# Where the pre-added weight blocks of a seven-product SwiGLU pair are made: accumulating DMA or VectorE

## The chip, the cores and the metric

One core of one Trainium2 chip runs the whole program. The metric is device time in microseconds. TensorE (PE) multiplies, VectorE (DVE) and ScalarE (ACT) do elementwise work, GpSimd (POOL) also issues the accumulating DMAs, and SyncE (SP) issues the plain ones.

## The reference

Two layers on x of 512 tokens by 1024 channels, each followed by a SwiGLU feed-forward network. The change lies in the latter alone:

```python
def swiglu_layer(x, norm_g, w_gate_up, w_down):
    h = rmsnorm(x, norm_g)
    g, u = jnp.split(h @ w_gate_up, 2, axis=-1)
    return x + (jax.nn.silu(g) * u) @ w_down
```

The hidden width is 2816, which is 22 blocks of 128 columns. A block m of gate columns with the same block of up columns is called a pair here.

## The kernel before

Activations lie with channels on partitions and the 512 tokens in the free dimension. Every product is made in three matmuls: a weight is split into a rounded high part (`whi`, a cast on ACT, L93) and a remainder (`wlo`, a subtraction on VectorE, L94), and so is the activation.

In each of the two feed-forward networks pairs 0 to 4 are multiplied plainly. Pairs 5 to 21 go through `seven`: gate and up weights of a pair are seen as a 2x2 block matrix (two halves of the 1024 input channels by gate and up), the tokens as two halves, and the 2x2 product is made with seven block products instead of eight, each 4 channel blocks by 3 matmuls of 256 columns, so 84 matmuls a pair. The blocks that are needed on the weight side are, with g and u the gate and up weights and 1 and 2 their halves along the channels:

- a1: g whole, as it comes (tile `raw`);
- s13: two sums side by side, u1 + u2 and u1 + g1;
- s24: (u1 + u2) + g1, and that + g2, made by two adds on VectorE (L143, L144; called add 2 and add 3 below) out of the first half of s13 and `raw`;
- a22: u2.

Each of the four is then split into high and low parts. `emit` asks for the pieces one pair ahead: the call of `seven` for pair m makes those of pair m+1. The 17 pairs are worked in three runs, 5 to 7, 8 to 14 and 15 to 21, and after each run comes the down projection of the hidden blocks made so far (8 output blocks of 512-column matmuls). The two longer runs of both networks are called stages A (pairs 8 to 14, first network), B (15 to 21), C and D (the same of the second network).

The wide buffers are few: four weight tiles named `raw` are shared by a pair's transfers and by the down projection's weights, five high/low pairs hold split weights. So a transfer waits until the buffer that it takes has been read to the end by the pair before the last. All waiting is on queues that work in order: SP issues the plain transfers in the order of the program, POOL the accumulating ones, and VectorE and ACT also take one instruction after another, so that one which waits holds up all behind it. That order is set by the framework's scheduler when the program is built.

In `seven` VectorE also takes products out of PSUM: u2 = r2 + s (L792) has to be read before the third group of products adds to the same bank, and likewise u3 (L799), then the outputs `tg` (L807), `tu` (L812, L813). PE takes the groups of a pair in the order a1, then the rest of the pair before (s24), s24, the rest of the pair before (a22), s13, s13, a1; a group of 12 matmuls each.

In a profile row the tile that holds s13 is named `raw` before the change, since it comes out of the same ring, and a22 is shown as `a`.

Of the kernel before, what the change touches and what calls it, by code (L numbers as in the profile page):

```python
# [10 lines left out]
F32 = mybir.dt.float32  # L11
# [3 lines left out]
ALU = mybir.AluOpType  # L15
AX = mybir.AxisListType

P = 128
# [7 lines left out]
KF = FF // P  # L26
# [3 lines left out]
NSTD = 5  # L30
# [31 lines left out]
def trunk(ctx: ExitStack, tc: tile.TileContext, a):  # L62
    nc = tc.nc
    mm = nc.tensor.matmul
    V, S, G = nc.vector, nc.scalar, nc.gpsimd
# [18 lines left out]
    WMAX = D  # L84
# [7 lines left out]
    def split(src, hi, lo, eng=V):  # L92
        S.copy(hi, src)  # L93
        eng.tensor_tensor(out=lo, in0=src, in1=hi.bitcast(F32), op=ALU.subtract)  # L94
# [4 lines left out]
    lent = {"stage": None, "pool": None, "raw": 0, "split": 0}  # L99

    def ring(what, stage):

        own, more = (NRAW, 1) if what == "raw" else (NSPL, 2)
        names = (("raw", F32),) if what == "raw" else (("whi", F32R), ("wlo", F32R))
        pool, bufs = wp, own
        if stage is not None and stage == lent["stage"]:
            lent[what] += 1
            if lent[what] % (own + more) >= own:
                pool, bufs = lent["pool"], more
        return [pool.tile([P, WMAX], dt, tag=n, bufs=bufs, name=n) for n, dt in names]  # L110

    parts = {}

    def emit(j):
        src, n, kind, stage = specs[j]
        HW = WMAX // 2
        if kind == "plain":
            raw, = ring("raw", stage)
            hi, lo = ring("split", stage)
            step = n if j else n // 4  # L120
            for c in range(0, n, step):
                nc.sync.dma_start(out=raw[:, c:c + step], in_=src[:, c:c + step])
                split(raw[:, c:c + step], hi[:, c:c + step], lo[:, c:c + step], G if src.tensor.name in on_pool else V)
        elif kind == "a1":

            g, u = src
            fp = lent["pool"]
            raw, = ring("raw", stage)
            s13, = ring("raw", stage)
            a22 = fp.tile([P, HW], F32, tag="a22", name="a22", bufs=2)  # L130
            for z in range(2):
                nc.sync.dma_start(out=s13[:, z * HW:(z + 1) * HW], in_=u[:, :HW])
            nc.sync.dma_start(out=raw, in_=g)
            nc.sync.dma_start(out=a22, in_=u[:, HW:])
            nc.gpsimd.dma_start(out=s13[:, :HW], in_=u[:, HW:], accum_op=ALU.add)  # L135
            nc.gpsimd.dma_start(out=s13[:, HW:], in_=g[:, :HW], accum_op=ALU.add)
            parts.update(raw=raw, s13=s13, a22=a22)
            hi, lo = ring("split", stage)
            split(raw, hi, lo)
        elif kind == "s24":  # L140
            raw, s13 = parts["raw"], parts["s13"]
            t = lent["pool"].tile([P, WMAX], F32, tag="s24", name="s24", bufs=1)
            V.tensor_tensor(out=t[:, :HW], in0=s13[:, :HW], in1=raw[:, :HW], op=ALU.add)  # L143
            V.tensor_tensor(out=t[:, HW:], in0=t[:, :HW], in1=raw[:, HW:], op=ALU.add)  # L144
            hi, lo = ring("split", stage)
            split(t, hi, lo)
        elif kind == "s13":
            hi, lo = ring("split", stage)
            split(parts["s13"], hi, lo)
        else:  # L150
            hi, lo = (lent["pool"].tile([P, HW], F32R, tag=f"a22{z}", name=f"a22{z}", bufs=1) for z in "hl")
            split(parts["a22"], hi, lo)
        w_of[j] = (hi, lo)

    def weight(i):
        while emitted[0] < len(specs) and emitted[0] <= i + (AHEAD if specs[emitted[0]][2] == "plain" else 4):
            emitted[0] += 1
            emit(emitted[0] - 1)
        return w_of.pop(i, None)
# [69 lines left out]
    def slot(i, dtype):  # L229
        return [xp.tile([P, T], dtype, tag=f"x{z}{i}", name=f"x{z}{i}") for z in "hl"]  # L230
# [79 lines left out]
    with ExitStack() as rctx:  # L310
# [63 lines left out]
        for c in range(NT):  # L374
# [33 lines left out]
            out=adt.rearrange("p (c h) -> p c h", c=NT),  # L408
            in0=dt.rearrange("p (c h) -> p c h", c=NT),
            scalar=-1.0,  # L410
            in1=ea.rearrange("p (o h) -> p o h", o=1).to_broadcast([P, NT, H]),
# [24 lines left out]
        for g in range(2):  # L436
# [7 lines left out]
            for c in range(NT):  # L444
                s = slice(c * P, (c + 1) * P)
# [3 lines left out]
                out=t.rearrange("p (c l) -> p c l", c=NT), in0=ps.rearrange("p (c l) -> p c l", c=NT),  # L449
                in1=tri.rearrange("p (o l) -> p o l", o=1).to_broadcast([P, NT, P]), op=ALU.mult,  # L450
# [245 lines left out]
        op = rctx.enter_context(tc.tile_pool(name="op", bufs=1))  # L696
# [9 lines left out]

    HOMES = [("F", i) for i in range(5)] + [("S", i) for i in (8, 9, 10, 11, 4, 5, 6, 7)] + [("F", i) for i in range(5)] + [("S", i) for i in (8, 9, 10, 11)]

# [4 lines left out]
    def ffn(norm, idx, after):  # L717
        l, gu, dn = idx
        HT = T // 2
        with ExitStack() as fctx:  # L720
            fp = fctx.enter_context(tc.tile_pool(name="fp", bufs=1))
# [47 lines left out]
            def finish(m, tu):  # L769
                z, i = HOMES[m]  # L770
                hi, lo = slot(i, F32R) if z == "S" else [fp.tile([P, T], F32R, tag=f"a{y}{i}", name=f"a{y}") for y in "hl"]
                split(tu, hi, lo)
                act[m] = (hi, lo)

            def small(tag):
                return fp.tile([P, HT], F32, tag=tag, name=tag, bufs=2)

            def seven(m, last):

# [2 lines left out]
                r1, r2 = (pa.tile([P, T], F32, tag="pa", name="ps_r")[:, :HT] for _ in range(2))  # L782
                r3 = pm.tile([P, T], F32, tag="pm", name="ps_r3")[:, :HT]
                s, u2, u3, m5 = small("s"), small("u2"), small("u3"), small("m5")
                a1 = weight(gu[m]["a1"])
                product(r1, a1, 0, "B11", True)
# [379 lines left out]
```

## Time and profile before

| | |
|---|---|
| median of 3 runs | 1334.52 us (1334.01 to 1335.09) |
| the profiled execution | 1333.48 us, of which the span 1331.6 us |
| PE busy | 1296.0 us, 97% of the span |
| VectorE busy | 928.1 us, 70% |
| ACT busy | 645.6 us, 48% |
| POOL busy | 180.0 us, 14% |
| granted TensorE clock, mean | 0.996 |
| accumulating DMAs issued by POOL | 68 of 256 KB, median 5.5 us to landing |
| plain DMAs of gate and up weights issued by SP | 54 of 512 KB at 3.6 us, 68 of 256 KB at 3.4 us, 34 of 256 KB at 3.9 us |

The span runs from the first to the last instruction. A share of busy time is a mean over stages with different limits, and idle time on an engine costs nothing unless another waits for it in the end. In the windows below the first row is the first run of pairs, and stages A to D follow; (x) is a count of instructions. A row's duration includes pipelining: matmuls start before the one ahead has ended, so the distance between starts tells the pace.

### The profile page before, as it was taken

Reading aid. Unit: us, or ns where it says so; the run is one execution under the profiler, and the core shown is the slowest. Engines: PE = TensorE matmul, PEld = TensorE weight load, DVE = VectorE, ACT = ScalarE, POOL = GpSimd, SP = SyncE. Lnnn points to the kernel's source line nnn. Section 1 sums busy time; section 2 is a strip of 40 time slices with the busy share of each in tenths; the row PEclk is TensorE's granted clock in tenths of the full one; section 3 lists DMA queues with packets and bytes.
Section 4 is the critical chain, followed back from the end, with each engine's and each line's share of the span. In section 5 each row is a group of like instructions: output and inputs, shape, how many; then the busy total and the mean of one; then the engine's idle time right before and its main releaser. Section 6 shows DMA issues by size and latency. Waiting matters only on the chain.

```text
span 1331.6 us, 18948 instructions
## 1 busy us (share of the span) xinstructions
PE 1296.0 (97%) x7346; PEld 1113.9 (84%) x7346; DVE 928.1 (70%) x1550; ACT 645.6 (48%) x1012; POOL 180.0 (14%) x178
## 2 busy tenths in 40 slices
PE   7999989999999999999999999999999999999998
PEld 6877767788889889889888877877878989889997
DVE  6886789975688558747764666777789746765772
ACT  6743858443455325424443467546654514433540
POOL 0000000000010111011104453354201011111100
PEclk9999989999999999999999999999999999999999
DMA  7323322532454646564632321221245554565541
GB/s 242 112 80 94 96 74 70 163 111 91 143 131 109 173 109 164 162 143 111 158 96 80 95 79 33 64 79 49 66 132 120 158 127 127 144 162 131 148 128 56
DMA packets 58154, 153.46 MB, mean 115 GB/s; under 512 B 6464, under 2 KB 7232, under 8 KB 57936
## 3 DMA queue, kind: packets, MB, share of 16 engines
q1 hardware_dynamic: 48272, 134.43, 32.7%
q0 software_dynamic: 9792, 17.83, 8.6%
q8 instruction: 57, 0.93, 0.3%
q14 instruction: 33, 0.27, 0.1%
HBM read 150.10 MB, written 2.13 MB: 114 GB/s over the span
## 4 chain that ended last, share of the span: by engine, by line
PE 81%; DVE 8%; ACT 4%; DMA 4%; issue 2%; SPq 0%; POOL 0%; DVEq 0%; ACTq 0%; POOLq 0%
PE ps_pr L163 15%; PE ps_pr L164 15%; PE ps_pr L165 15%; PE ps_r L765 6%; PE ps_r L767 6%; PE ps_r L766 6%; DMA raw<-in_w_gu 4%; PE ps_qkv L905 3%; PE ps_qkv L906 3%; PE ps_qkv L907 3%; DVE wlo L94 3%; PE ps_pT L1017 1%; ACT s L996 1%; PE ps_s L988 1%; PE ps_o L1025 1%
## 5 line engine op out<-in xcount | busy, mean ns | idle before, releaser
L93 ACT CAST whi<-raw 128x1024 fp32r<-128x1024 f32 (+2 forms) x223 | 227.4, 1022 | 327.1 <-PE ps_pr L165 208.8
L163 PE MATMUL ps_pr<-xh,wlo 128*128 128x512 f32 x704 | 279.7, 397 | 13.0 <-DVE wlo L94 12.3
L164 PE MATMUL ps_pr<-xl,whi 128*128 128x512 f32 x704 | 277.7, 394 | 0.6 <-DVE xl L245 0.6
L165 PE MATMUL ps_pr<-xh,whi 128*128 128x512 f32 x704 | 276.6, 393 | 0.0
L94 DVE TENSOR_TENSOR wlo<-raw,whi 128x1024 fp32r<-128x1024 f32 (+2 forms) x191 | 224.4, 1181 | 42.1 <-ACT whi L93 41.2
L163 PEld LDWEIGHTS ps_pr<-xh,wlo 128*128 128x128 f32 x704 | 133.5, 190 | 42.4 <-DVE wlo L94 13.1
L164 PEld LDWEIGHTS ps_pr<-xl,whi 128*128 128x128 f32 x704 | 133.4, 189 | 29.7 <-DVE xl L245 1.8
L165 PEld LDWEIGHTS ps_pr<-xh,whi 128*128 128x128 f32 x704 | 133.3, 189 | 28.6 <-issue 0.6
L840 DVE TENSOR_TENSOR x<-ps_pr,x 128x512 f32<-128x512 f32 x48 | 33.2, 691 | 96.8 <-PE ps_pr L165 96.6
L94 POOL TENSOR_TENSOR wlo<-raw,whi 128x1024 fp32r<-128x1024 f32 x32 | 78.0, 2438 | 167.1 <-ACT whi L93 167.1
L135 POOL DMA_DIRECT2D raw<-in_w_gu x34 | 30.4, 893 | 482.8 <-DMA raw<-in_w_gu 191.8
L765 PE MATMUL ps_r<-xh,wlo 128*128 128x256 f32 x272 | 77.1, 283 | 0.0
L767 PE MATMUL ps_r<-xh,whi 128*128 128x256 f32 x272 | 77.0, 283 | 0.0
L766 PE MATMUL ps_r<-xl,whi 128*128 128x256 f32 x272 | 77.0, 283 | 0.0
L907 PE MATMUL ps_qkv<-whi,xh 128*128 128x512 f32 x192 | 75.5, 393 | 0.0
L905 PE MATMUL ps_qkv<-whi,xl 128*128 128x512 f32 x192 | 75.4, 392 | 0.0
L906 PE MATMUL ps_qkv<-wlo,xh 128*128 128x512 f32 x192 | 75.3, 392 | 0.0
L93 ACT CAST whi<-s 128x1024 fp32r<-128x1024 f32 x34 | 35.8, 1052 | 71.2 <-PE ps_pr L165 37.4
L143 DVE TENSOR_TENSOR s<-raw 128x512 f32<-128x512 f32 x34 | 23.5, 691 | 56.3 <-DMA raw<-in_w_gu 54.5
L163 PE MATMUL ps_pr<-ah,wlo 128*128 128x512 f32 x160 | 62.3, 389 | 0.0
L164 PE MATMUL ps_pr<-al,whi 128*128 128x512 f32 x160 | 62.3, 389 | 0.0
L165 PE MATMUL ps_pr<-ah,whi 128*128 128x512 f32 x160 | 62.2, 389 | 0.0
(372 smaller groups left out, 3074.7 us busy)
## 6 DMA issues: line engine op xcount, KB each, us to landing
raw<-in_w_gu SPq DMA_DIRECT2D x54, 512.0 KB, 3.6
raw<-in_w_in SPq DMA_DIRECT2D x35, 512.0 KB, 3.6
raw<-in_w_gu SPq DMA_DIRECT2D x68, 256.0 KB, 3.4
raw<-in_w_gu POOLq DMA_DIRECT2D x68, 256.0 KB, 5.5
raw<-in_w_dn SPq DMA_DIRECT2D x32, 448.0 KB, 3.9
raw<-in_w_qkv SPq DMA_DIRECT2D x24, 512.0 KB, 3.5
a<-in_w_gu SPq DMA_DIRECT2D x34, 256.0 KB, 3.9
raw<-in_w_out SPq DMA_DIRECT2D x16, 512.0 KB, 3.6
```

The costliest lines, as they stand in the source:

```text
L93: S.copy(hi, src)
L94: eng.tensor_tensor(out=lo, in0=src, in1=hi.bitcast(F32), op=ALU.subtract)
L163: mm(ps, lhsT=wl[ws], rhs=xh[xs], start=start, stop=False)
L164: mm(ps, lhsT=wh[ws], rhs=xl[xs], start=False, stop=False)
L165: mm(ps, lhsT=wh[ws], rhs=xh[xs], start=False, stop=stop)
L765: mm(ps, lhsT=wl[:, c:c + P], rhs=fh, start=first and k == 0, stop=False, skip_group_check=not first)
L766: mm(ps, lhsT=wh[:, c:c + P], rhs=fl, start=False, stop=False, skip_group_check=not first)
L767: mm(ps, lhsT=wh[:, c:c + P], rhs=fh, start=False, stop=k == 3, skip_group_check=not first)
L840: V.tensor_tensor(out=x[m], in0=ps, in1=x[m], op=ALU.add)
L905: mm(pss[t], lhsT=xl[:, ts_], rhs=wh[:, cols], start=(k == 0), stop=False)
L906: mm(pss[t], lhsT=xh[:, ts_], rhs=wl[:, cols], start=False, stop=False)
L907: mm(pss[t], lhsT=xh[:, ts_], rhs=wh[:, cols], start=False, stop=(k == KD - 1))
```

## The change

The sum u1 + u2 is made on VectorE out of a plain transfer of the whole u tile (`up`, from the same ring as `raw`); the accumulating DMA is left for u1 + g1 alone. The s13 tile has two buffers of its own. The add on VectorE is called add 1. u2 has no buffer of its own any more: a22 is the second half of `up`, which is therefore held until a22 has been split. To make room, a pair of hidden blocks fewer is kept in that pool (`HOMES` tells in which buffer a hidden block lies) and three small tiles have one buffer instead of two.

```diff
         elif kind == "a1":
 
             g, u = src
-            fp = lent["pool"]
             raw, = ring("raw", stage)
-            s13, = ring("raw", stage)
-            a22 = fp.tile([P, HW], F32, tag="a22", name="a22", bufs=2)
-            for z in range(2):
-                nc.sync.dma_start(out=s13[:, z * HW:(z + 1) * HW], in_=u[:, :HW])
+            up, = ring("raw", stage)
+            s13 = lent["pool"].tile([P, WMAX], F32, tag="s13", name="s13", bufs=2)
+            nc.sync.dma_start(out=s13[:, HW:], in_=u[:, :HW])
             nc.sync.dma_start(out=raw, in_=g)
-            nc.sync.dma_start(out=a22, in_=u[:, HW:])
-            nc.gpsimd.dma_start(out=s13[:, :HW], in_=u[:, HW:], accum_op=ALU.add)
+            nc.sync.dma_start(out=up, in_=u)
             nc.gpsimd.dma_start(out=s13[:, HW:], in_=g[:, :HW], accum_op=ALU.add)
-            parts.update(raw=raw, s13=s13, a22=a22)
+            a22 = up[:, HW:]
+            parts.update(raw=raw, s13=s13, a21=up[:, :HW], a22=a22)
             hi, lo = ring("split", stage)
             split(raw, hi, lo)
         elif kind == "s24":
             raw, s13 = parts["raw"], parts["s13"]
+            V.tensor_tensor(out=s13[:, :HW], in0=parts["a21"], in1=parts["a22"], op=ALU.add)
             t = lent["pool"].tile([P, WMAX], F32, tag="s24", name="s24", bufs=1)
...
-    HOMES = [("F", i) for i in range(5)] + [("S", i) for i in (8, 9, 10, 11, 4, 5, 6, 7)] + [("F", i) for i in range(5)] + [("S", i) for i in (8, 9, 10, 11)]
+    NF = NSTD - 1
+    HOMES = [("F", i) for i in range(NF)] + [("S", i) for i in (8, 9, 10, 11, 4, 5, 6, 7)] + [("F", i) for i in range(3)]
+    HOMES += [("S", i) for i in (8, 9, 10, 11)] + [("F", i) for i in range(NF)]
+    assert len(HOMES) >= KF
...
             def small(tag):
-                return fp.tile([P, HT], F32, tag=tag, name=tag, bufs=2)
+                return fp.tile([P, HT], F32, tag=tag, name=tag, bufs=2 if tag == "s" else 1)
```

The scheduler puts the instructions in another order. The first place is SP's queue in stage A, where it issues for pairs 12 to 14. Before, L133 is a gate tile (raw_4619 and raw_4754 are those of pairs 13 and 14), L132 the two halves of s13 (raw_4485, raw_4620 and raw_4755: pairs 12, 13 and 14), L134 a22:

```order
L134 DMA a22_4351<-in_w_gu 128x512
L132 DMA raw_4485<-in_w_gu 128x512 x2
L132 DMA raw_4620<-in_w_gu 128x512 x2
L134 DMA a22_4486<-in_w_gu 128x512
L133 DMA raw_4754<-in_w_gu 128x1024
L133 DMA raw_4619<-in_w_gu 128x1024
L134 DMA a22_4621<-in_w_gu 128x512
L132 DMA raw_4755<-in_w_gu 128x512 x2
```

In the same place of the changed program L131 is a gate tile (raw_4611 and raw_4745 for pairs 13 and 14), L132 the whole up tile (raw_4344, raw_4478, raw_4612 and raw_4746: pairs 11 to 14), and L130 the u1 half that the accumulating DMA then adds to:

```order
L131 DMA raw_4477<-in_w_gu 128x1024
L132 DMA raw_4344<-in_w_gu 128x1024
L130 DMA s13_4479<-in_w_gu 128x512
L132 DMA raw_4478<-in_w_gu 128x1024
L131 DMA raw_4611<-in_w_gu 128x1024
L130 DMA s13_4613<-in_w_gu 128x512
L131 DMA raw_4745<-in_w_gu 128x1024
L132 DMA raw_4612<-in_w_gu 128x1024
L130 DMA s13_4747<-in_w_gu 128x512
L132 DMA raw_4746<-in_w_gu 128x1024
```

A pair's three plain transfers take the place of four, and the whole up tile of a pair is issued before or after its neighbour's gate tile, as its buffer comes free.

The second place is VectorE's queue at the end of the same stage, where the last pair's s24 is made (add 2 and add 3 of pair 14 are L143 and L144) beside the split of pair 13's s13 (wlo_4698):

```order
L143 TENSOR_TENSOR s24_4794<-raw_4755,raw_4754 128x512
L94 TENSOR_TENSOR xl6_4694<-tu_4476,xh6_4693 128x512
L799 TENSOR_TENSOR u3_4617<-ps_r_4613,s_4615 128x256
L144 TENSOR_TENSOR s24_4794<-s24_4794,raw_4754 128x512
L800 TENSOR_TENSOR tu_4611<-m5_4618,u3_4617 128x256
L94 TENSOR_TENSOR wlo_4798<-s24_4794,whi_4797 128x1024
L94 TENSOR_TENSOR wlo_4698<-raw_4620,whi_4697 128x1024
L807 TENSOR_TENSOR tg_4610<-ps_r3_4614,u2_4616 128x256
L94 TENSOR_TENSOR wlo_4764<-raw_4754,whi_4763 128x1024
```

After the change add 1 of pair 14 is L140, add 2 and add 3 are L142 and L143, and wlo_4689 is the split of pair 13's s13:

```order
L94 TENSOR_TENSOR a22l_4586<-raw_4478,a22h_4585 128x512
L814 TENSOR_TENSOR tu_4469<-ps_r_4471,s_4473 128x256
L815 SCALAR_TENSOR_TENSOR tu_4469<-tu_4469,tg_4468 128x512
L140 TENSOR_TENSOR s13_4747<-raw_4746 128x512
L801 TENSOR_TENSOR u3_4609<-ps_r_4605,s_4607 128x256
L94 TENSOR_TENSOR xl7_4685<-tu_4469,xh7_4684 128x512
L802 TENSOR_TENSOR tu_4603<-m5_4610,u3_4609 128x256
L142 TENSOR_TENSOR s24_4784<-s13_4747,raw_4745 128x512
L143 TENSOR_TENSOR s24_4784<-s24_4784,raw_4745 128x512
L94 TENSOR_TENSOR wlo_4689<-s13_4613,whi_4688 128x1024
L94 TENSOR_TENSOR wlo_4788<-s24_4784,whi_4787 128x1024
L809 TENSOR_TENSOR tg_4602<-ps_r3_4606,u2_4608 128x256
```

The add that waits for a transfer is now add 1, it stands further ahead of the splits, and pair 13's s13 is split ahead of pair 14's s24 instead of behind it.

## Rows read from the trace of the kernel before

**Rows 1.** The page, busy time of TensorE over the whole span
```profile
PE 1296.0 (97%) x7346; PEld 1113.9 (84%) x7346; DVE 928.1 (70%) x1550; ACT 645.6 (48%) x1012; POOL 180.0 (14%) x178
```

**Rows 2.** Windows (start:end, length, busy PE, PEld, DVE, ACT, POOL, clock, DMA, GB/s)
```profile
413.20:443.43 30.23, 30.23 (x253) 30.23 (x252) 23.53 (x34) 17.00 (x26) 0.00 (x0) 1.00 0.43 126
486.98:560.20 73.22, 71.05 (x589) 70.64 (x588) 55.10 (x85) 37.94 (x61) 7.04 (x8) 1.00 0.58 150
598.31:673.69 75.38, 72.27 (x589) 70.97 (x588) 54.87 (x85) 37.49 (x61) 7.07 (x8) 1.00 0.51 131
1101.41:1177.27 75.86, 72.96 (x590) 72.14 (x589) 55.08 (x85) 37.40 (x61) 7.07 (x8) 0.98 0.54 137
1215.37:1289.69 74.32, 71.82 (x589) 70.80 (x588) 55.02 (x85) 38.02 (x61) 7.06 (x8) 1.00 0.58 144
```

**Rows 3.** Timeline of TensorE: first matmul of a run, first one after it
```profile
413.20 0.28 PE L765 MATMUL ps_r<-b110h,wlo 128*128 128x256 f32 x1
...
443.43 0.40 PE L163 MATMUL ps_pr<-ah,wlo 128*128 128x512 f32 x1
```

**Rows 4.** Timeline, stage A: pair 14's pieces, until TensorE goes on
```profile
527.04 2.35 DVE L94 TENSOR_TENSOR wlo<-raw,whi 128x1024 fp32r<-128x1024 f32 x2
...
528.28 0.80 SPq L132 DMA_DIRECT2D raw<-in_w_gu  x2
...
531.53 0.89 POOL L135 DMA_DIRECT2D raw<-in_w_gu  x1 [16.34 <-DVE tu L812]
...
536.64 0.69 DVE L143 TENSOR_TENSOR s<-raw 128x512 f32<-128x512 f32 x1 [3.72 <-DMA raw<-in_w_gu]
537.25 0.68 DVE L94 TENSOR_TENSOR xl<-tu,xh 128x512 fp32r<-128x512 f32 x1
...
538.98 1.05 ACT L93 CAST whi<-s 128x1024 fp32r<-128x1024 f32 x1 [5.73 <-PE ps_r L767]
539.93 1.04 ACT L93 CAST whi<-raw 128x1024 fp32r<-128x1024 f32 x1
...
541.20 1.22 DVE L94 TENSOR_TENSOR wlo<-raw,whi 128x1024 fp32r<-128x1024 f32 x1
542.33 0.42 DVE L807 TENSOR_TENSOR tg<-ps_r,u 128x256 f32<-128x256 f32 x1
542.47 0.39 PE L765 MATMUL ps_r<-t00h,wlo 128*128 128x256 f32 x1 [2.06 <-DVE wlo L94]
542.67 1.21 DVE L94 TENSOR_TENSOR wlo<-raw,whi 128x1024 fp32r<-128x1024 f32 x1
```

**Rows 5.** What VectorE waited for in stages A, B, C, D
```profile
DVE s L143 <- DMA raw<-in_w_gu: 8.5, 4, 3.7
DVE wlo L94 <- ACT whi L93: 4.1, 8, 0.9
...
DVE s L143 <- DMA raw<-in_w_gu: 12.7, 4, 5.4
...
DVE s L143 <- DMA raw<-in_w_gu: 10.9, 4, 4.5
...
DVE s L143 <- DMA raw<-in_w_gu: 10.7, 4, 4.8
```

**Rows 6.** Window in stage C in which the granted clock was lower
```profile
1149.50:1152.90 3.40, 3.40 (x17) 3.19 (x16) 2.05 (x5) 0.89 (x2) 0.00 (x0) 0.50 0.77 243
```

**Rows 7.** The line of the 512 KB gate transfers, and that of add 2
```profile
DMA to landing us min/median/max: 3.4/3.9/6.6
...
L143 DVE TENSOR_TENSOR s<-raw x34: 680/692/694, 398.1 to 1267.1; 128x512 f32<-128x512 f32 x34
```

**Rows 8.** Timeline of VectorE ahead of the first run of pairs
```profile
391.64 0.69 DVE L830 TENSOR_TENSOR tu<-ps_pr,nrb 128x512 f32<-128x512 f32 x1 [0.59 <-PE ps_pr L165]
...
413.40 0.69 DVE L830 TENSOR_TENSOR tu<-ps_pr,nrb 128x512 f32<-128x512 f32 x1 [0.91 <-PE ps_pr L165]
...
416.54 0.41 DVE L792 TENSOR_TENSOR u<-ps_r,s 128x256 f32<-128x256 f32 x1
```

## The prediction

> **What bounds the kernel now.** I read the page's busy times first. TensorE is busy for 1296.0 us of 1331.6, so some 35 us are open at most by that line [rows 1]. Next I looked for the stages in which it loses them, with the starts of its matmuls. The first run of three pairs goes from 413.20 to 443.43 without a gap: 30.23 us for 3 x 84 = 252 matmuls, 0.120 us each, 10.08 us a pair [rows 2, 3]. Seven pairs at that pace are 70.54 us. The four stages of seven pairs take 73.22, 75.38, 75.86 and 74.32 us [rows 2]: 2.68 + 4.84 + 5.32 + 3.78 = 16.6 us too much. That is all that a change of how the weight blocks are made can give back here.
>
> What the stages wait for I read from stage A's timeline [rows 4]. A split of s13 frees its buffer (VectorE's two subtractions from 527.04), SP issues the two u1 halves of pair 14 at 528.28, POOL the first accumulate at 531.53, once they have landed, and add 2 of pair 14 can start at 536.64: 8.4 us from SP's issue, behind an idle VectorE. Behind add 2 stands add 3, then ACT's cast of s24 at 538.98, and only behind that, in ACT's order, the cast of pair 13's s13 at 539.93, its subtraction at 541.20, and TensorE at 542.47 after 2.06 us of idleness. VectorE's waits for transfers at add 2 are 8.5, 12.7, 10.9 and 10.7 us in the stages, 42.8 us in 16 waits, 2.7 us each [rows 5]. In stage C such a wait also brings a stretch of 3.4 us at a granted clock of 0.50 (1.2 GHz instead of 2.4) [rows 6], half of which is lost; it is part of the 16.6 us.
>
> **The change part by part.** *The accumulate ahead of s24 goes.* s24 then needs only plain transfers. The accumulate that is left feeds the second half of s13, and that is split about two pairs after its buffer came free, 20 us, against the 8.4 us that both transfers took above: nothing is late there. I cost it at nothing; without that cover it would be the stall of rows 4 again.
>
> *What is late next* is `up`. By the changed program's waits it takes the buffer that one of three VectorE instructions frees (split of a22, split of a1, or add 3, of an earlier pair), is issued by SP at once unless another transfer ahead of it in the queue waits, and lands, if it behaves like the gate tile of the same size, 3.9 us later [rows 7]. VectorE meanwhile works on what its order puts between. At the pace of the rows, 0.60 us for a 512-column instruction (536.64 to 537.25), 1.13 for a split of 1024, 0.34 for 256 columns (541.20, 542.33, 542.67) [rows 4], that is, for pairs 11 to 14 in A and C and 18 to 21 in B and D, five times 3.1 us, three times 1.3, twice 2.4, twice 3.4, twice 4.6, once 2.2 and once 3.0. So add 1 waits five times 0.8, three times 2.6, twice 1.5, twice 0.5, twice not at all, once 1.7, once 0.9: 18.4 us in place of 42.8. Queued behind a waiting add 1 are u3, the outputs' split, add 2 and add 3, and the split of s13 or a1; the first that TensorE needs is s13's subtraction, 5.8 us into its pair, and u2, 7.2 us into it.
>
> What these waits cost TensorE is not in the trace, so from both sides. Nothing, if they end inside VectorE's slack: I put stage A's instructions of the changed order one behind another with these durations, and each split and u2 came before TensorE's need, the nearest by 0.4 us (u2 of pair 13). At the most, in proportion as before: 16.6 / 42.8 = 0.39 us of TensorE time for one of VectorE's waiting, 0.39 x 18.4 = 7.1 us. I take the middle, 3.6 us, since the transfers won't all land in 3.9.
>
> *34 more adds.* Each is an add like L143, 0.69 us [rows 7]. In the stages VectorE is busy for (55.10 + 54.87 + 55.08 + 55.02) / 28 = 7.86 us a pair [rows 2]; with the add 8.55 of 10.08. Its waits for ACT's casts, at the most-loaded kind of stage 4.1 us or 0.6 a pair [rows 5], leave about 0.9 us. So the adds lie beside TensorE's work, and cost nothing as long as add 1 waits for no more than that on average. Ahead of the first run of each network VectorE is nearly full: add 1 of three pairs and an a22 split that moves ahead are 4 x 0.6 = 2.4 us, against idle pieces of 0.59 and 0.91 [rows 8], so up to 0.9 us late at u2 of pair 5. That u2 starts at 416.54 and TensorE needs it by 417.5 (a run's first pair has nothing of a pair before it between its groups, so the group that needs u2 read begins after three groups of 12 matmuls: 413.20 + 3 x 1.44), done at 416.95 [rows 8]. Between 0 and 0.9 us I take 0.2, near to nothing, twice: 0.4 us.
>
> *The rest* costs nothing: u2, u3 and m5 with one buffer are read by VectorE half a pair before they are written again; the hidden blocks' new homes were all read by an earlier down projection; SP issues one transfer less per pair and POOL one of two.
>
> The sum, against the profiled execution's 1333.48 us: - 16.6 + 3.6 + 0.4 = - 12.6, so 1320.9. The median of the runs is 1.04 us above that execution: 1322 us.
>
> The Trainium skill ("Perfetto Trace Analysis", section "Identifying the Most-Contended Engine") holds that matmul occupancy is a poor measure of how much TensorE has left, because pipelined instructions look smaller in a trace. By occupancy the four stages hold 2.17 + 3.11 + 2.90 + 2.50 = 10.7 us of idleness, by the pace of starts 16.6 us [rows 2]; by the first the sum would be 1328, by the second it is 1322. The trace agrees with the rule in that a slow matmul counts as busy: the 3.4 us at half clock are wholly busy [rows 6].
>
> **Rivals.** *Slower: VectorE sets the pace of a pair.* Place: add 1, in the 16 pairs whose `up` waits for a buffer. 18.4 us of waits are 1.15 a pair against 0.9 of slack. Were `up`, queued with the half tiles and the gate tiles, to land after 5.25 us, halfway from the median to the longest of the gate transfers [rows 7], the waits would be 38.6 us, 2.4 a pair, 1.5 over the slack: 16 x 1.5 = 24 us lost in place of 16.6, so 1342. It decides from about 5.0 us on. For it speaks that transfers did take up to 6.6 us and that the stretch of rows 6 moves 243 GB/s; against, that fewer bytes are moved in a pair and that slack taken in one pair is partly given back in the next.
>
> *No change: the wait only moves.* A pair still takes two of four buffers, and `up` is held until a22 is split, later than s13 was. If add 1 waits as long as add 2 did, 2.7 us, the stages stay as they are: 1335. For it: the period of two pairs from buffer to buffer is the same. Against it: the path loses one of its two transfers in series, and at the end of stage A pair 13's s13 no longer stands behind pair 14's s24.
>
> *Half of it.* Only the idle pieces come back, and matmuls that started late without showing as idle stay: 10.7 - 4.0 = 6.7 us, 1328. For it: stalls at u2 and u3 come from VectorE's load, which grows. Against it: in the first run, with the same evacuations and no wait for transfers, there are none [rows 2].
>
> **How the numbers follow.** The forecast, 1322, has 0.60; its own range goes from 1318 (nothing given back) to 1327 (7.1 + 1.8 given back). Half of it has 0.16, no change 0.11, slower 0.13. Runs of this kernel differ by about 0.1% from their median, so 0.2%, 2.7 us, is what tells a change. Faster: 0.76, within 0.2%: 0.11, slower: 0.13. The range that is to hold it 8 times in 10 goes from 1317 to 1335: it takes in the case of no change and leaves out the slower one and a little below.
>
> **What would show it.** In the profile after: stages of seven pairs within 70.5 to 72.5 us each; no wait for transfers at the line of add 2; waits at add 1 of 10 to 25 us in sum; 34 accumulating DMAs; 23 us more VectorE time; no stretch at half clock in stage C. I am wrong if add 1 waits over 2 us each time, if `up` lands later than 5 us, or if TensorE waits for u2 or the split of s13 as long as now.

## The result

The changed kernel takes 1325.37 us (median of 4, 1324.07 to 1325.91) against 1334.8 us for the kernel before beside it, a ratio of 0.992 with a 95% interval of 0.9895 to 0.9945. It is faster, by some 9 us where 12.5 were forecast. Run again on another occasion the ratio was 0.9922 (0.9904 to 0.9941). The profiled execution is 1325.75 us, its span 1323.8.

The page's first rows: VectorE has 23.0 us more than in [rows 1] and 34 instructions more, GpSimd 30.2 us less.

```profile
PE 1293.1 (98%) x7346; PEld 1112.3 (84%) x7346; DVE 951.1 (72%) x1584; ACT 645.0 (49%) x1012; POOL 149.8 (11%) x144
...
s<-in_w_gu POOLq DMA_DIRECT2D x34, 256.0 KB, 5.3
```

The windows of the changed kernel, columns as in [rows 2]: the first run of pairs and stages A to D, and then the down projections that stand behind the first run of the first and of the second network.

```profile
414.38:444.61 30.23, 30.23 (x254) 30.23 (x252) 23.95 (x35) 17.02 (x26) 2.05 (x3) 1.00 0.58 152
488.16:561.38 73.22, 71.30 (x589) 70.69 (x588) 57.73 (x88) 37.31 (x61) 5.23 (x6) 1.00 0.50 134
599.49:670.55 71.06, 70.80 (x589) 70.59 (x588) 57.72 (x89) 37.87 (x61) 3.46 (x4) 1.00 0.46 127
1100.19:1172.46 72.27, 71.07 (x589) 70.66 (x588) 58.12 (x89) 37.92 (x61) 5.20 (x6) 1.00 0.53 139
1210.57:1281.69 71.12, 70.81 (x590) 70.61 (x588) 56.94 (x87) 37.28 (x61) 3.51 (x4) 1.00 0.47 128
...
444.61:488.16 43.55, 43.55 (x195) 36.04 (x194) 21.58 (x27) 8.93 (x10) 0.86 (x1) 1.00 0.39 116
1054.84:1100.19 45.35, 44.13 (x195) 35.97 (x193) 24.23 (x29) 11.36 (x14) 0.88 (x1) 1.00 0.38 111
```

Against 70.54 us for seven pairs the stages now lose 2.68 + 0.52 + 1.73 + 0.58 = 5.5 us instead of 16.6: 11.1 are won, and stage C stays at a granted clock of 1.00. Stage A lasts 73.22 us, as long as before to the hundredth, which is chance: in a second profile of the changed kernel (e_again below) it lasts 72.64. And a down projection that took 43.54 us before (its window below) takes 45.35: 1.8 us are given back there. With 1.2 us of a later first pair and 0.3 us elsewhere, - 11.1 + 1.8 + 1.2 + 0.3 is the - 7.8 between the two spans.

```profile
1057.87:1101.41 43.54, 43.54 (x194) 36.04 (x193) 19.50 (x24) 8.95 (x10) 5.34 (x6) 1.00 0.59 148
```

What VectorE and TensorE waited for in stages A, B, C and D of the changed kernel (us in total, times, longest). Add 2 has no wait left.

```profile
PE ps_r L767 <- DVE u L794: 1.9, 3, 1.4
DVE s L140 <- DMA raw<-in_w_gu: 3.0, 3, 1.4
...
PE ps_r L767 <- DVE u L794: 0.3, 1, 0.3
DVE s L140 <- DMA raw<-in_w_gu: 4.2, 3, 3.0
...
PE ps_r L767 <- DVE u L794: 1.2, 2, 0.7
DVE s L140 <- DMA raw<-in_w_gu: 4.7, 3, 2.6
...
PE ps_r L767 <- DVE u L794: 0.3, 1, 0.3
DVE s L140 <- DMA raw<-in_w_gu: 3.1, 1, 3.1
```

15.0 us at add 1 (L140) stand where 42.8 stood at add 2 [rows 5]. TensorE now waits at one line alone, u2 (L794). How it comes about is seen in stage A, pairs 12 to 14, VectorE's timeline and TensorE's:

```profile
529.43 0.69 DVE L140 TENSOR_TENSOR s<-raw 128x512 f32<-128x512 f32 x1 [1.12 <-DMA raw<-in_w_gu]
...
533.96 1.23 DVE L94 TENSOR_TENSOR wlo<-s,whi 128x1024 fp32r<-128x1024 f32 x1 [0.83 <-ACT whi L93]
...
537.34 0.69 DVE L140 TENSOR_TENSOR s<-raw 128x512 f32<-128x512 f32 x1 [0.49 <-DMA raw<-in_w_gu]
...
540.55 2.48 DVE L94 TENSOR_TENSOR wlo<-s,whi 128x1024 fp32r<-128x1024 f32 x2
542.95 0.42 DVE L809 TENSOR_TENSOR tg<-ps_r,u 128x256 f32<-128x256 f32 x1
543.28 1.22 DVE L94 TENSOR_TENSOR wlo<-raw,whi 128x1024 fp32r<-128x1024 f32 x1
544.41 0.42 DVE L794 TENSOR_TENSOR u<-ps_r,s 128x256 f32<-128x256 f32 x1
...
544.88 0.39 PE L767 MATMUL ps_r<-t10h,wlo 128*128 128x256 f32 x1 [1.37 <-DVE u L794]
```

Three short waits push the queue back; from 537.34 on VectorE works without a gap, and u2 of pair 13 stands at its end. TensorE goes on 1.37 us late.

The lost time of the down projection has another cause. In it ACT waits for a down-projection weight, and the last hidden block's split stands behind that cast:

```profile
1046.73 0.86 POOL L133 DMA_DIRECT2D s<-in_w_gu  x1 [7.23 <-DMA s<-in_w_gu]
...
1047.29 0.33 SPq L122 DMA_DIRECT2D raw<-in_w_dn  x1
...
1053.95 1.05 ACT L93 CAST whi<-raw 128x1024 fp32r<-128x1024 f32 x1 [3.96 <-DMA raw<-in_w_dn]
...
1060.79 0.51 PE L162 MATMUL ps_pr<-xh,wlo 128*128 128x512 f32 x1 [0.99 <-ACT xh L93]
```

The transfer of 1047.29 lands after 6.6 us, at 1053.9; GpSimd issued an accumulate 0.6 us ahead of it. In the first network the accumulate comes 1.4 us behind the same transfer (438.42 and 437.06), this lands in 3.5 us, and nothing is lost; the weight after it, issued at 439.46, 1.0 us behind the accumulate, lands in 5.3 us.

### The profile page after: what moved, and what is told of

It reads as the page before. It is cut to its first block, busy times and chain, and to the rows that moved or that the text cites. A ratio compares the mean times of both kernels' runs of the same rounds, so it can differ in the third digit from the quotient of the medians.

```text
span 1323.8 us, 18869 instructions
## 1 busy us (share of the span) xinstructions
PE 1293.1 (98%) x7346; PEld 1112.3 (84%) x7346; DVE 951.1 (72%) x1584; ACT 645.0 (49%) x1012; POOL 149.8 (11%) x144
## 4 chain that ended last, share of the span: by engine, by line
PE 81%; DVE 8%; ACT 5%; DMA 4%; issue 2%; SPq 0%; POOL 0%; DVEq 0%; ACTq 0%
PE ps_pr L162 15%; PE ps_pr L163 15%; PE ps_pr L164 15%; PE ps_r L767 6%; PE ps_r L769 6%; PE ps_r L768 6%; DMA raw<-in_w_gu 3%; PE ps_qkv L907 3%; PE ps_qkv L908 3%; PE ps_qkv L909 3%; DVE wlo L94 2%; PE ps_pT L1019 1%; ACT s L998 1%; ACT whi L93 1%; PE ps_s L990 1%
## 5 line engine op out<-in xcount | busy, mean ns | idle before, releaser
L93 ACT CAST whi<-raw 128x1024 fp32r<-128x1024 f32 (+2 forms) x189 | 191.6, 1017 | 307.2 <-PE ps_pr L164 181.9
L94 DVE TENSOR_TENSOR wlo<-raw,whi 128x1024 fp32r<-128x1024 f32 (+2 forms) x157 | 184.0, 1174 | 43.9 <-ACT whi L93 43.1
L163 PEld LDWEIGHTS ps_pr<-xl,whi 128*128 128x128 f32 x704 | 133.7, 190 | 30.2 <-DVE xl L244 1.8
L93 ACT CAST whi<-s 128x1024 fp32r<-128x1024 f32 x68 | 71.4, 1050 | 87.5 <-PE ps_pr L164 50.9
L133 POOL DMA_DIRECT2D s<-in_w_gu x34 | 30.0, 891 | 597.8 <-DMA s<-in_w_gu 154.2
L94 DVE TENSOR_TENSOR wlo<-s,whi 128x1024 fp32r<-128x1024 f32 x68 | 83.1, 1223 | 19.5 <-ACT whi L93 19.2
```

Of the source, the lines that this page charges most:

```text
L163: mm(ps, lhsT=wh[ws], rhs=xl[xs], start=False, stop=False)
```

## The experiments

In the table a stage's loss is its length in the windows less 70.54 us; the waits are those of VectorE for a transfer at add 1 (at add 2 where add 1 isn't there) in the four stages (7.4 us of those of e_bufs are put down to issue by the profile). Ratios are to the kernel before, run beside each; its median was 1331.6 us beside the first four experiments, 1335.19 beside the next and 1334.59 beside the last, so ratios are compared and not times.

| kernel | ratio, 95% interval | lost in A, B, C, D | waits |
|---|---|---|---|
| before | 1 | 2.7, 4.8, 5.3, 3.8 | 42.8 |
| changed | 0.992 (0.9895 to 0.9945) | 2.7, 0.5, 1.7, 0.6 | 15.0 |
| e_again | 0.9922 (0.9904 to 0.9941) | 2.1, 0.5, 2.4, 0.3 | 14.3 |
| e_bufs | 1.0284 (1.0261 to 1.0308) | 11.5, 12.4, 11.2, 11.3 | 72.2 |
| e_inplace | 0.9929 (0.9915 to 0.9943) | 0.6, 3.3, 0.9, 0.4 | 15.2 |
| e_twice | 0.998 (0.9969 to 0.999) | 0.6, 1.3, 6.0, 1.5 | 16.2 |
| e_pool3 | 1.0212 (1.0191 to 1.0232) | 5.9, 10.8, 10.1, 8.5 | 0.0 (63.2 on GpSimd) |
| e_ring5 | 0.9888 (0.987 to 0.9906) | 0.0, 0.6, 0.0, 0.0 | 8.1 |
| e_noacc | 0.9882 (0.9863 to 0.99) | 0.4, 0.0, 1.0, 0.0 | 6.3 |
| e_ipg | 0.9903 (0.9885 to 0.9921) | 1.4, 1.1, 0.0, 1.8 | 2.5 |
| e_noacc2 | 0.9876 (0.9853 to 0.9898) | 0.0, 0.5, 0.0, 0.0 | 5.2 |
| e_ring5v | 0.9893 (0.9873 to 0.9914) | 0.0, 0.0, 0.0, 0.7 | 2.7 (2.6 more at u1 + g1) |

**Accumulate or buffers?** The theory is that the gain is the accumulate taken out of the path of s24; the rival, that it is the new buffers.

e_bufs has the changed kernel's buffers and both accumulates:

```diff
-            nc.sync.dma_start(out=s13[:, HW:], in_=u[:, :HW])
+            for z in range(2):
+                nc.sync.dma_start(out=s13[:, z * HW:(z + 1) * HW], in_=u[:, :HW])
...
-            nc.sync.dma_start(out=up, in_=u)
+            nc.sync.dma_start(out=up[:, HW:], in_=u[:, HW:])
+            nc.gpsimd.dma_start(out=s13[:, :HW], in_=u[:, HW:], accum_op=ALU.add)
...
-            V.tensor_tensor(out=s13[:, :HW], in0=parts["a21"], in1=parts["a22"], op=ALU.add)
```

> The changed kernel's buffers, homes and small tiles, but both sums by accumulating DMA as before (no add 1; u1 into both halves of s13, u2 alone into its half of up). Theory (the gain is the accumulate taken out of the path of s24): the stages lose about 16.7 us again, VectorE waits 35 to 45 us at add 2, the time is 1332 to 1337. Rival (the gain is the buffers: s13 no longer shares the ring): it stays at 1324 to 1327, with 5 to 8 us lost in the stages.

1368.01 us: neither. The stages lose 46.3 us, nearly three times what they lost before. A stall of it in stage A:

```profile
529.71 0.86 POOL L134 DMA_DIRECT2D s<-in_w_gu  x1 [11.68 <-DVE a22l L94]
...
534.28 0.69 DVE L143 TENSOR_TENSOR s<-s,raw 128x512 f32<-128x512 f32 x1 [4.02 <-DMA s<-in_w_gu]
```

SP issued that pair's u1 halves at 525.97; 8.3 us later add 2 starts. The chain of two transfers is as long as in [rows 4], but VectorE waits 72.2 us for it in the four stages instead of 42.8. So the buffers by themselves are no gain; why they cost so much, I did not follow further.

e_inplace keeps the buffers of before and replaces only the one accumulate:

```diff
-            nc.gpsimd.dma_start(out=s13[:, :HW], in_=u[:, HW:], accum_op=ALU.add)
...
+            V.tensor_tensor(out=s13[:, :HW], in0=s13[:, :HW], in1=parts["a22"], op=ALU.add)
```

> The kernel before with its own buffers; only the accumulate of u2 is replaced by an add on VectorE that works in place on the first half of s13 (u1 + a22). Theory (accumulate path): 1321 to 1328, stages lose 3 to 8 us. Rival (buffers): 1332 to 1337, no gain.

0.9929, the changed kernel's gain in full, and no loss in the down projection (43.55 us). The theory holds: one line of the change is worth all of it. That line also takes 256 KB of traffic away in each pair, and the scheduler orders the queues anew. From 480 to 675 us u1 lands after 3.2 us (median) instead of 3.7 and a22 after 3.3 instead of 4.0; both gains are small against the 5.4 us of the accumulate that is gone, but no run parts the shares.

**What still costs: VectorE's load, or the landing of `up`?** After the timeline of stage A my theory was that VectorE's queue is full.

e_twice:

```diff
-            V.tensor_tensor(out=s13[:, :HW], in0=parts["a21"], in1=parts["a22"], op=ALU.add)
+            for z in range(2):
+                V.tensor_tensor(out=s13[:, :HW], in0=parts["a21"], in1=parts["a22"], op=ALU.add)
```

> The changed kernel with add 1 made twice (the second writes the same values again), 0.69 us more of VectorE per pair. Theory (what is still lost in stages A and C is VectorE's packed queue ahead of u2): each of the some 16 adds that stand inside the stages adds up to 0.69 us there, half of them inside slack: 1328 to 1336. Rival (it is the landing of up that still costs, VectorE has slack): within 1 us of the changed kernel, 1324.5 to 1326.5.

1329.23 us, 0.998: some 0.6% or 8 us above the changed kernel, as the theory had it. Its stages lose 9.4 us where the changed kernel's lose 5.3 to 5.5, so about half of that is seen in them. e_pool3 takes all three adds off VectorE:

```diff
-            V.tensor_tensor(out=s13[:, :HW], in0=parts["a21"], in1=parts["a22"], op=ALU.add)
+            G.tensor_tensor(out=s13[:, :HW], in0=parts["a21"], in1=parts["a22"], op=ALU.add)
...
-            V.tensor_tensor(out=t[:, :HW], in0=s13[:, :HW], in1=raw[:, :HW], op=ALU.add)
-            V.tensor_tensor(out=t[:, HW:], in0=t[:, :HW], in1=raw[:, HW:], op=ALU.add)
+            G.tensor_tensor(out=t[:, :HW], in0=s13[:, :HW], in1=raw[:, :HW], op=ALU.add)
+            G.tensor_tensor(out=t[:, HW:], in0=t[:, :HW], in1=raw[:, HW:], op=ALU.add)
```

> The changed kernel with adds 1 to 3 on GpSimd. By rows of GpSimd's subtractions (2.44 us for 1024 columns) an add is about 1.2 us, three 3.7 us per pair, and VectorE gets 1.38 us per pair less than before and has no wait for up in its queue. Theory (VectorE's queue): u2 is never late, the stages lose under 2 us, 1318 to 1322. Rival (the landing of up limits, and s24 now comes 3.7 instead of 2.1 us behind it): 1326 to 1334. Second rival (GpSimd and VectorE slow each other): VectorE's adds or splits get longer than now and the time is above 1328.

1360.7 us. Its stage B, GpSimd, VectorE and TensorE's waits:

```profile
635.74 1.29 POOL L140 TENSOR_TENSOR s<-raw 128x512 f32<-128x512 f32 x1 [5.23 <-DMA raw<-in_w_gu]
637.11 1.29 POOL L142 TENSOR_TENSOR s<-s,raw 128x512 f32<-128x512 f32 x1
638.48 1.26 POOL L143 TENSOR_TENSOR s<-s,raw 128x512 f32<-128x512 f32 x1
...
640.85 1.23 DVE L94 TENSOR_TENSOR wlo<-s,whi 128x1024 fp32r<-128x1024 f32 x1 [6.04 <-ACT whi L93]
...
643.12 0.42 DVE L794 TENSOR_TENSOR u<-ps_r,s 128x256 f32<-128x256 f32 x1
...
PE ps_r L767 <- DVE u L794: 6.7, 2, 4.9
```

VectorE doesn't wait at the adds any more, but at the split of s24, 6.04 us, and u2 is queued behind that. The adds can leave the queue; the wait comes back into it one step later, and longer. The time is far beyond the first rival's range; the second rival's signs are there. The split of s24 and s13 takes up to 2321 ns where it took 1228 at most in the changed kernel, and an add on GpSimd takes 1.45 to 1.72 us on average instead of 1.2. And the four stages hold seven stretches, 26.9 us together, at a granted clock of 0.50 to 0.53; half of that, some 13 of the 35 us lost, is the clock. How the rest divides between the two rivals isn't shown.

e_ring5 lets the transfers go earlier (in place, five raw buffers and three for a22; homes and small tiles as in the changed kernel to make the room):

```diff
-        own, more = (NRAW, 1) if what == "raw" else (NSPL, 2)
+        own, more = (NRAW, 2) if what == "raw" else (NSPL, 2)
...
-            a22 = fp.tile([P, HW], F32, tag="a22", name="a22", bufs=2)
+            a22 = fp.tile([P, HW], F32, tag="a22", name="a22", bufs=3)
```

> The add in place in the buffers of before, with one more raw buffer (5 instead of 4) and a third a22 buffer, in the room that the changed kernel's fewer homes and small tiles give. Theory (add 1 waits because its transfer waits for a buffer, and what is left is lost behind that wait): waits at add 1 under 8 us in the four stages, stages lose under 2.5 us, ratio 0.987 to 0.991. Rival (VectorE's load alone makes u2 late): as with four buffers, 0.992 to 0.994, 4 to 6 us lost.

0.9888; the stages lose 0.6 us, three of the four last 70.55 to 70.56, with waits of 8.1 us where under 8 were expected. VectorE does no less work than in e_inplace (58.0 to 58.7 us a stage against 57.8 to 58.0), so its load was not what cost. e_noacc takes the other road: u1 + g1 on VectorE too, no accumulating DMA and no u1 transfer.

```diff
-            nc.sync.dma_start(out=s13[:, HW:], in_=u[:, :HW])
...
-            nc.gpsimd.dma_start(out=s13[:, HW:], in_=g[:, :HW], accum_op=ALU.add)
...
+            V.tensor_tensor(out=parts["s13"][:, HW:], in0=parts["a21"], in1=parts["raw"][:, :HW], op=ALU.add)
             hi, lo = ring("split", stage)
             split(parts["s13"], hi, lo)
```

> The changed kernel with u1 + g1 on VectorE too, out of up and raw: no accumulating DMA and no u1 transfer at all, 256 KB and an accumulate less per pair, 0.69 us of VectorE more. Theory (VectorE's slack is used up): it costs about what a repeated add 1 cost, ratio 0.995 to 1.000, with more than 8 us lost in the stages; the 1.8 us of the down projection are not lost. Rival (the accumulating DMA and its traffic make up land late, and that is what is still lost): 0.988 to 0.992.

0.9882: my theory of a full VectorE falls, and its rival holds. With one more add per pair the stages lose 1.5 us instead of 5.3. What differs is when `up` lands. The line of its transfers and who waited for it, 480 to 675 us, changed kernel and then e_noacc:

```profile
  DVE s L140: 8.8, 8
...
DMA to landing us min/median/max: 3.5/4.5/5.0
```

```profile
  DVE s L138: 5.1, 4
...
DMA to landing us min/median/max: 3.4/3.5/4.0
```

e_noacc2 makes add 1 twice in e_noacc, by the edit of e_twice:

> The kernel with all sums on VectorE, with add 1 made twice (same values): VectorE at some 9.1 us of a pair's 10.08 in the stages, with no accumulating DMA. Theory (waits at add 1 and instructions draw on one slack, which the shorter waits leave): 2 to 6 us above the same kernel without the repeat, ratio 0.990 to 0.993, where the repeat cost the changed kernel some 7 us. Rival (only the waits matter): within 1 us, 0.988 to 0.989. Second rival (VectorE sets the pace at once): over 8 us, above 0.994.

0.9876, no slower than e_noacc. Its stage C:

```profile
1095.16:1165.71 70.55, 70.55 (x589) 70.55 (x588) 61.86 (x97) 38.46 (x61) 0.00 (x0) 1.00 0.32 95
```

VectorE is busy for 61.86 of 70.55 us, and TensorE loses nothing. So instructions alone do not make u2 late here; waits do. Why the repeat did cost in e_twice isn't fully explained: its waits were long as well (16.2 us), and its loss lies mostly in stage C, where waits at add 1 came to 6.2 us. There TensorE stood still for 1.91 us waiting for u2, and then ran for 3.4 us at a granted clock of 0.51 (1.2 GHz), which makes up some 1.7 of that stage's 6.0 us:

```profile
1156.00:1159.40 3.40, 3.40 (x19) 3.40 (x18) 3.31 (x6) 2.14 (x4) 0.09 (x1) 0.51 0.93 196
```

**The accumulating DMA, or the bytes?** e_ipg is e_inplace with the sum of u1 + g1 on GpSimd; its plain transfers are the same, and only the accumulating DMA is gone.

```diff
-            nc.gpsimd.dma_start(out=s13[:, HW:], in_=g[:, :HW], accum_op=ALU.add)
...
+            G.tensor_tensor(out=parts["s13"][:, HW:], in0=parts["s13"][:, HW:], in1=parts["raw"][:, :HW], op=ALU.add)
```

> The add in place in the buffers of before, with u1 + g1 as an add on GpSimd in place of the accumulating DMA. Theory (that sum has about 20 us, so its way is free; GpSimd's adds stretch VectorE's instructions beside them by some 0.2 us): 0.993 to 0.998, a22's split longer than 0.69 us on average. Rival (accumulating traffic delays the plain transfers): 0.989 to 0.992.

0.9903. The waits at add 1 fall from 15.2 to 2.5 us, and a22 lands in 2.6 us (median, at most 3.2) instead of 3.3 (at most 5.2) in 480 to 675 us. So the plain transfers land earlier without the accumulating DMA beside them. But GpSimd's adds lengthen VectorE's work: the split of a22, e_inplace and then e_ipg,

```profile
L94 DVE TENSOR_TENSOR a22l<-a,a22h 128x512 fp32r<-128x512 f32 x34 | 23.3, 684 | 0.0
```

```profile
L94 DVE TENSOR_TENSOR a22l<-a,a22h 128x512 fp32r<-128x512 f32 x34 | 31.4, 923 | 0.0
```

and what the waits gave goes again. Two more runs were to part accumulate from bytes, with the transfers put back into a tile that nobody reads: e_traffic the plain one, e_accidle the accumulate too.

```diff
+            idle = lent["pool"].tile([P, HW], F32, tag="idle", name="idle", bufs=1)
+            nc.sync.dma_start(out=idle, in_=u[:, :HW])
             nc.sync.dma_start(out=raw, in_=g)
             nc.sync.dma_start(out=up, in_=u)
+            nc.gpsimd.dma_start(out=idle, in_=g[:, :HW], accum_op=ALU.add)
```

> The kernel with all sums on VectorE (no accumulating DMA), with the plain 256 KB u1 transfer put back into a tile that nobody reads. Theory (it is the accumulating DMA, not the bytes, that makes the transfers of up and of the down projection's weights land late): ratio 0.987 to 0.990, median landing of up 3.5 to 3.9 us, no loss in the down projections. Rival (the bytes do it): ratio 0.990 to 0.993, up lands in 4.2 to 4.6 us as in the changed kernel.

> The same with the accumulate onto that unread tile as well: the changed kernel's transfers in full, but no instruction waits for their result. Theory (accumulating traffic slows the others): ratio 0.991 to 0.995, up lands in 4.2 to 4.6 us, 4 to 8 us lost in the stages, and the down projection behind the first run of the second network again takes 45 us or more. Rival (what cost in the changed kernel was waiting for s13, not traffic): 0.987 to 0.990.

0.9896 (0.9876 to 0.9916) and 1.0293 (1.0269 to 1.0317), and neither tells it: since nobody reads the tile, the scheduler put the transfers elsewhere. Whether the accumulation or its 256 KB delays the others stays open. The transfers of e_traffic are all issued ahead of the first runs (the first network's 17 from 358.2 to 410.0), and with e_accidle GpSimd is busy for 0.00 us in its four stages, which lose 1.1 us together. Its time goes into the first runs, 51.9 and 52.2 us instead of 30.2:

```profile
424.27 7.61 SPq L131 DMA_DIRECT2D idle<-in_w_gu  x2
431.98 0.37 SPq L133 DMA_DIRECT2D raw<-in_w_gu  x1
...
435.97 0.69 DVE L141 TENSOR_TENSOR s<-raw 128x512 f32<-128x512 f32 x1 [15.10 <-DMA raw<-in_w_gu]
```

SP waits until an accumulate has landed before it may fill the tile again, `up` stands behind that in SP's queue, and add 1 waits 15.10 us: a queue held up by a transfer that no one needs.

**Again, and both together.** e_again is the changed kernel unaltered.

> The changed kernel as it is, beside the others on one chip. Ratio to before 0.990 to 0.994. If the 1.8 us that the down projection behind the first run of the second network lost come from an order of transfers that is fixed in the program (accumulate of pair 8 against a down-projection weight), that stretch is 45.2 to 45.5 us again; if from chance, 43.5 us. The first run of pairs starts 0 to 1.2 us from where it starts before.

0.9922; the first run of pairs starts at 413.29, so the later start of the first profile was chance. The down projection is not: 47.24 us this time, beyond the 45.2 to 45.5 expected, again with ACT's wait for the weight, 4.26 us. It is issued 0.6 us behind an accumulate as before and lands in 6.9 us. Of the 3.7 us some 1.7 come from another stretch at a granted clock of 0.51, behind TensorE's wait of 1.28 us:

```profile
1060.40:1063.80 3.40, 3.40 (x10) 2.65 (x9) 1.92 (x2) 1.04 (x1) 0.00 (x0) 0.51 0.13 53
```

In e_inplace no accumulate is issued between 1040 and 1056 us, the weights there land in 3.5 to 4.7 us, and the down projection takes 43.55 us, as it does in e_noacc.

e_ring5v is e_ring5 with u1 + g1 on VectorE, in place:

```diff
-            nc.gpsimd.dma_start(out=s13[:, HW:], in_=g[:, :HW], accum_op=ALU.add)
...
+            V.tensor_tensor(out=parts["s13"][:, HW:], in0=parts["s13"][:, HW:], in1=parts["raw"][:, :HW], op=ALU.add)
```

> A version to beat both: all sums on VectorE, in place, in five raw buffers and three a22 buffers. If longer ahead and less traffic add up, the stages lose under 1 us and the down projections nothing: ratio 0.985 to 0.989; if VectorE's load begins to show, 0.989 to 0.992.

0.9893: no better than either alone, as there is under 2 us left in the stages. e_noacc beats both kernels: its interval ends at 0.99, that of the changed kernel beside it begins at 0.9904; e_ring5 comes close with 0.9888, but its interval just touches that of the changed kernel.

## Why the prediction was right

- **The bound.** The four stages' 16.6 us were all there was to win, by the pace of starts; 11.1 came back, and the experiments' best come to 16.0. By occupancy there were 10.7 us of idleness, less than what was won.
- **The accumulate ahead of s24.** Right, and shown by itself (e_inplace): the whole gain hangs on it. One reading was off. u1 had landed 2.6 us after 528.28, at 530.9, and the accumulate of 531.53 was held up to then by VectorE, by its own row [rows 4]. So the 8.4 us are 2.6 of transfer, some 0.6 of waiting for VectorE and 5.1 of accumulate.
- **What is late next.** Right in place: `up` at add 1, and behind it u2, of pair 13 in stage A before all, which I had 0.4 us ahead of TensorE's need. The waits are 15.0 us against 18.4, but that they came so near is luck: `up` landed after 4.2 us (median from 414 to 1290 us; 4.5 in A and B) instead of the 3.9 taken from the gate tile before, and with 4.2 the prediction's own list of gaps gives 22.6 us. So the gaps were taken too short on the whole. The cost to TensorE is 5.5 us against 3.6, inside the bounds of 0 and 7.1. That is 0.37 us for one of VectorE's waiting, nearly the 0.39 of before; the middle that was taken, 0.20, was too low. The point from which VectorE would set the pace, 5.0 us, was set for a rival that e_noacc2 takes away: VectorE bears more.
- **34 more adds.** No cost, right. But I had all of them in the stages: only 16 of 28 stand there, the others are made during the down projections, so VectorE has (57.73 + 57.72 + 58.12 + 56.94) / 28 = 8.23 us a pair and not 8.55.
- **0.4 us in the first runs.** Not there: both last 30.23 us.
- **"The rest costs nothing."** This is the step that failed. I counted one transfer less on SP and one of two on GpSimd as free, and did not ask what else they meet. The remaining accumulate now goes out just ahead of a down-projection weight, and that costs 1.8 us (3.7 in the second profile, half clock included) in a stretch where TensorE had not waited before.
- **The signs.** The waits, the 34 accumulating DMAs, VectorE's 23 us and the clock in stage C came as stated; stage A, at 73.22 us, lies outside the 70.5 to 72.5 stated for each stage.

The sum of the terms was - 12.6 us; - 11.1 + 1.8 are - 9.3, and the medians of the result are 9.4 apart. So close an agreement is luck: for e_again the same sum is - 16.6 + 5.3 + 3.7 = - 7.6, and the medians there are 9.8 apart. The rival "half of it" forecast 1328, and by the number alone it is no further from 1325.4 than the forecast of 1322. It has the right idea of u2, and TensorE's idle pieces in the stages did fall by 7.0 us, from 10.7 to 3.7, near its 6.7. But the stages got 11.1 us shorter, so time that did not show as idle came back too, which the rival ruled out. That the waits only move holds for stage A alone.

## What to carry to other kernels

An accumulating DMA in front of an add is two transfers in a row, and all that is queued behind the waiting add pays; where the engine has room, make the sum there. Ask of what is left of such DMAs which plain transfers they meet, also outside the stage that is changed. And test "the engine is full" by giving it more work: here a stage took 61.86 us of VectorE without loss, where shorter waits were worth 4 us.

## What the runs showed of the hardware

Plain transfers land later behind or beside an accumulating DMA: down-projection weights issued 0.6 us behind one took 6.6 and 6.9 us, and 3.5 us where it came 1.4 us after the weight; a22's longest landing was 5.2 us with it and 3.2 us without. A plain transfer of the same size in its place was not measured. And GpSimd's adds lengthen VectorE's. The line of the product of the two outputs (two inputs in SBUF; min/median/max in ns), e_inplace and then e_ipg:

```profile
L813 DVE SCALAR_TENSOR_TENSOR tu<-tu,tg x34: 684/692/694, 427.7 to 1280.5; 128x512 f32<-128x512 f32 x34
```

```profile
L813 DVE SCALAR_TENSOR_TENSOR tu<-tu,tg x34: 679/692/1654, 426.5 to 1279.1; 128x512 f32<-128x512 f32 x34
```

The longest becomes 1654 ns, while u3, which reads one input from PSUM, stays at 426 ns at most. The sum behind it, of m5 and u3 (two inputs in SBUF), stays at 426 ns too in e_ipg. In e_pool3, with more adds on GpSimd, it reaches 1518 ns, while u3 stays at 425:

```profile
L801 DVE TENSOR_TENSOR u<-ps_r,s x34: 409/425/425, 421.6 to 1313.3; 128x256 f32<-128x256 f32 x34
L802 DVE TENSOR_TENSOR tu<-m,u x34: 424/426/1518, 422.1 to 1313.9; 128x256 f32<-128x256 f32 x34
```

The Trainium skill ("SBUF — State Buffer", section "Who interferes with whom") says that a VectorE instruction with two inputs in SBUF contends with a GpSimd instruction that reads SBUF, and one with at most one SBUF input, outside the two-port modes, does not; these rows agree, though they do not show how often u3 ran beside such an add.
